# Rotated queries and keys of retention heads 1 to 3 from seven block products, and another order of the first loads

## The chip, the cores and the metric

The program runs on one core of one Trainium2 chip. Its time is the device time of one execution in microseconds (us). The core has a matrix engine (TensorE, PE in the profile; loading its stationary operand is PEld), VectorE (DVE), ScalarE (ACT), GpSimd (POOL) and SyncE (SP). SP, ACT and POOL issue the transfers between main memory and the on-chip memory; these run on 16 DMA engines. Matmul results go to PSUM, which is used here as eight tiles of 128 x 512 floats.

## The reference, cut to what matters

Two layers run over 512 tokens of width 1024. Each has a token-mixing part (dilated attention and a retention, both from one input projection of 11648 columns) and a feed-forward part. The change touches the queries and keys of the retention, four heads with 256 query and 256 key columns each:

```python
z = jnp.einsum('bsd,dc->bsc', x, w_in) + b_in          # the projection, 1024 deep
...
def rot(t):                                            # t: [B, S, H, 256]
    t1, t2 = t[..., :half], t[..., half:]
    return jnp.concatenate([t1 * cos - t2 * sin, t1 * sin + t2 * cos], axis=-1)
q = rot(q)
k = rot(k) * (dk ** -0.5)
...
sc = jnp.einsum('bhnd,bhmd->bhnm', qc, kc) * decay_mask
```

cos and sin depend on the token and on the index in the half (128 values). All of it is in float32.

## The kernel before, in words

**Numbers in two parts.** A float32 operand is held as a rounded high part and a low part that is the rest. `hilo` makes them: ACT casts the high part (L93), DVE subtracts it from the source for the low part (L94). A product of two such operands is three matmuls (`mm3`, all of them on L82): high by high, high by low, low by high. The input x stands transposed in `xh` and `xl`, eight blocks of 128 channels by 512 tokens; weights go from `raw` buffers (eight of 128 x 1024) into pairs `whi` and `wlo` (four of each).

**Direct products.** `wstat` makes 128 columns for all 512 tokens: eight channel blocks, three matmuls with 512 moving columns each. Its weights are cast by `unit` (L93, L94).

**Block products.** `Right`, `tall` and `wide` compute two column blocks from two weight blocks with seven products of half the depth and half the tokens in place of eight (Strassen's scheme in Winograd's form). x is cut in two halves of channels and two of tokens; sums of its blocks (S1 to S4) are made once per layer into `xs`. Of the weights, four blocks B11, B12, B21, B22 are combined: P1 and P3 are a load (SP) and then a transfer that adds a second block to it, issued by POOL (L321, `accum_op`), P2 and P4 are additions on DVE (L347). Each of the seven right operands is cast on ACT (L330) and subtracted on DVE (L336). `tall` has x stationary and 512 weight columns moving; `wide` has the weights stationary and 256 tokens moving, 24 matmuls to a product. After each product `ev(i, ps)` is called, which takes the partial results together. Three products accumulate in turn in one PSUM tile ("A" chain), so a later product there waits until the `ev` before it has read it:

```python
CHAIN = {1: "A", 6: "A", 7: "A", 4: "A", 2: "X", 5: "C", 3: "C"}
FIRST = (1, 2, 5)
WIDE = tuple(ORDER[i] for i in (0, 2, 4, 1, 5, 3, 6))   # products 1, 5, 6, 2, 7, 3, 4
```

`wide` is used before the change for the two branch gates and for most of the feed-forward part, `tall` for the values and gates of the retention.

**Retention.** For each head h: `rotary(h)` makes queries and keys (four `wstat`, L664) and rotates them on DVE (L668, L672, L673); `ret_values_gates(h)` is a `tall` of 512 value and 512 gate columns. Between the matmuls `tick` takes jobs from a list `side`: during `rotary(h)` the outputs of head h-1 (`one`: matmuls, a norm, then `turn`: transposes, a copy and a store), during values and gates the scores of head h. `one` needs a reciprocal root, for which POOL computes a power (L125) between two DVE instructions (L124, L126). `pace(20)` spreads the list over 20 us of estimated matmul time; `drain` runs what is left.

**The order of the work.** The program's text gives priorities; the order of each engine's instructions and of each queue is fixed when the kernel is built, by a planner that looks for what is ready by its own estimates of durations. On the chip each queue then runs in that fixed order.

**The start (layer 0).** Three warming matmuls; SP loads x in four tiles of 128 tokens and the first weights; x is transposed on PE (L170). The first matmuls (`wstat_halves`, tokens 0 to 255 first) need x tiles 0 and 1 and the first weights. POOL loads small tables, then cos and sin (L758, L759), then bias rows (L448, L451).

Of the kernel before, what the change touches and what calls it, by code (L numbers as in the profile page):

```python
# [14 lines left out]
ALU = mybir.AluOpType  # L15
# [38 lines left out]
def hybrid_kernel(ctx, tc, x, rel_bias, w_in, b_in, w_attn_proj, w_ret_proj, w_out,  # L54
# [582 lines left out]
    def layer(ly, cp):  # L637
# [16 lines left out]
        def slot(name="op", dt=F32R):  # L654
            return opp.tile([P, 2, S], dt, tag="op", name=name)

        def rotary(h):

            rot = []
            for c0 in (C_QR + h * RQ, C_KR + h * RQ):  # L660
                us = pair_units(w_l, c0)
                prod = []
                for t in range(2):
                    ps = wstat(us, t)  # L664
                    pr = []
                    for tb in (cos, sin):
                        m = work("rp")
                        dve.scalar_tensor_tensor(out=m, in0=ps, scalar=bcol(c0 + t * P), in1=tb, op0=ALU.add, op1=ALU.mult)  # L668
                        pr.append(m)
                    prod.append(pr)  # L670
                (t1c, t1s), (t2c, t2s) = prod
                dve.tensor_tensor(out=t1c, in0=t1c, in1=t2s, op=ALU.subtract)  # L672
                dve.tensor_tensor(out=t1s, in0=t1s, in1=t2c, op=ALU.add)  # L673
                pair = []
                for src in (t1c, t1s):
                    o_ = slot("rot")
                    hilo(src, o_[:, 0], o_[:, 1])
                    pair.append(o_)
                rot.append(pair)
            heads[h]["q"], heads[h]["k"] = rot  # L680

        def ret_values_gates(h):
            cv, cg = C_VR + h * RV, C_GR + h * RV
# [18 lines left out]
        with stage("attn") as ap_, stage("attw", 4) as aw:  # L702
            qk = {}

            def qk_slot(hp, g):
                qk[hp, g] = opp.tile([P, 2, S], F32, tag="op", name="qk")

            def qk_units(hp, g, how=pair_units):
                c = g * GW + hp * P
                return how(w_l, C_QA + c, C_KA + c)  # L710

            def qk_put(hp, g, j, ps):
                cc = (C_QA, C_KA)[j] + g * GW + hp * P
                o_, i_ = qk[hp, g][:, j], ps
                if g:
                    o_ = o_.rearrange("p (r l) -> p r l", r=4)
                    i_ = i_.rearrange("p (l r) -> p r l", r=4)
                dve.tensor_scalar(o_, i_, bcol(cc), (HD ** -0.5, 1.0)[j], op0=ALU.add, op1=ALU.mult)

            if ly == 0:  # L720
                x0 = [slot("x0", F32) for _ in range(NI)]
                warm = work("warm")
                dve.memset(warm, 0.0)
                px = psum()

                for _ in range(WARM):
                    mm(px, warm[:, :P], warm, True, True)
                act.dma_start(ident, c_id)

                def load_x(i):  # L730
                    for hf in range(2):
                        nc.sync.dma_start(x0[i][:, hf], x[i * P:(i + 1) * P, hf * S:(hf + 1) * S])

                load_x(0)
                load_x(1)
                for l_ in range(DEPTH):
                    pool.dma_start(braws[l_], b_in[l_].rearrange("(a b) -> a b", b=P))
                vecs = bias_vectors([aw.tile([P, S], F32, tag="bias", name="hot") for _ in range(NG)])
                first, make = qk_units(0, 0, pair_apart)
                load_x(2)  # L740
                cp = x_copies()
                late = []
                ops = [to_xT(x0[i].rearrange("p a b -> p (a b)"), i, cp, late if i < 2 else None) for i in range(NI)]
                for f in ops[0] + ops[1]:
                    f()
                make()
                for f in late:
                    f()
                us0 = [first, qk_units(0, 1)]
                load_x(3)  # L750
                side.extend([lambda l_=l_: bias_cols(l_) for l_ in range(DEPTH)] + vecs[:3] + ops[2] + vecs[3:] + ops[3])
                dve.tensor_tensor(out=pick, in0=ident[:, :NR], in1=ident[:, BK:BK + NR], op=ALU.add)
                rate[0], credit[0] = 0.4, 0.0
            else:
                us0 = [qk_units(0, g) for g in range(2)]
            for g in range(NG):
                qk_slot(0, g)
            pool.dma_start(cos, c_cos)  # L758
            pool.dma_start(sin, c_sin)  # L759
            if ly == 0:  # L760
                bias_rows()
            pss = wstat_halves([(us, j) for us in us0 for j in range(2)])
            drain()
            side.extend(x_sums(cp))
            pace(8)
            for n_, ps in enumerate(pss):
                qk_put(0, n_ // 2, n_ % 2, ps)
            us = qk_units(0, 2)
            for j in range(2):
                qk_put(0, 2, j, wstat(us, j))  # L770
            for t in range(2):
                c1, c2 = C_VA + t * VB, C_VA + (2 + t) * VB

                def put(i, s, c):
                    nc.sync.dma_start(v_d[i * P:(i + 1) * P, c - C_VA:c - C_VA + VB], s)

                def left(i, ps, s, c1=c1):
                    if s is None:
                        s = work("sn")[:, :VB]
                        act.copy(out=s, in_=ps)  # L780
                    else:
                        dve.tensor_tensor(out=s, in0=ps, in1=s, op=ALU.add)
# [24 lines left out]

            bias, tail = {}, []
            load_bias(0)
            for hp in range(HPG // 2):  # L810
                if hp:
                    for g in range(NG):
                        us = qk_units(hp, g)
                        qk_slot(hp, g)
                        for j in range(2):
                            qk_put(hp, g, j, wstat(us, j))
                    drain()
                ops, t_ = attention_pair(hp, [qk[hp, g] for g in range(NG)], load_v(hp), ap_, bias, yaT)
# [12 lines left out]
            for _ in range(4):  # L831
                next(vg)
            drain()

        with stage("ret") as rp:
            def ret_scores(h):
# [5 lines left out]
                def one(j):  # L842
                    n = S - j * P
                    ps = psum()[:, :n]
                    for d in range(2):
                        k_, q_ = heads[h]["k"][d], heads[h]["q"][d]
                        mm3(ps, k_[:, 0, j * P:(j + 1) * P], k_[:, 1, j * P:(j + 1) * P],
                            q_[:, 0, j * P:], q_[:, 1, j * P:], d == 0, d == 1)
                    t = work("pt")
                    dve.tensor_tensor(out=t[:, :n], in0=ps, in1=dec[:, :n], op=ALU.mult)  # L850
                    sl = heads[h]["p"][j]
# [354 lines left out]
```

## Time and profile before

| | |
|---|---|
| median of three runs | 2185.17 us (2185.1 to 2186.9) |
| the profiled execution | 2185.52 us, of it a span of 2183.7 us from first to last instruction |
| granted TensorE clock, mean | 0.997 |
| PE busy | 2161.5 us, 99% of the span |
| DVE busy | 1396.0 us, 64% |
| ACT busy | 980.6 us, 45% |
| POOL busy | 228.3 us, 10% |
| main memory read, written | 310.67 MB, 28.53 MB |

Busy times are sums of the durations of an engine's instructions where they overlap counted once. A matmul's record is longer than the distance to the next one, since they are pipelined: what a matmul costs in a run of them is read from the distance of their starts. Rows of the timeline give start, duration, engine, line, operation, output and inputs, and in brackets the idle time before it with what ended it. A row of the windows gives busy time and count for PE, PEld, DVE, ACT and POOL, then clock, DMA share and GB/s.

### The profile page before, as it was taken

The numbers are of one execution on the slowest core, as the hardware profiler recorded it, in microseconds if no ns is written. First come the engines' busy times: TensorE is split into PE (matmuls) and PEld (weight loads), VectorE is DVE, ScalarE is ACT, GpSimd is POOL, SyncE is SP. The second block draws the span as 40 slices with busy tenths as digits, with TensorE's granted clock in tenths as the row PEclk, the third lists the DMA queues.
The fourth block names the chain that finished last, engine by engine and source line by source line (L and its number), as shares of the span: only waits on it lengthen the run. The fifth ranks groups of instructions, "written<-read, shape, count | busy, mean of one in ns | idle before, by whom it ended". The sixth has DMA issues, their size and how long they took to land.

```text
span 2183.7 us, 32442 instructions
## 1 busy us (share of the span) xinstructions
PE 2161.5 (99%) x12906; PEld 1902.4 (87%) x12906; DVE 1396.0 (64%) x2011; ACT 980.6 (45%) x1585; POOL 228.3 (10%) x253
## 2 busy tenths in 40 slices
PE   8999999999999999999999999999999999999998
PEld 7977788889988899989898778888899889999996
DVE  5643677777755685747675346767877447766575
ACT  4444544546633263525245445444556233544350
POOL 4100011011000100010020000111010001000001
PEclk9999999999999999999999999999999999999999
DMA  8944266458685356656269343565577762666551
GB/s 230 235 134 104 59 164 164 135 131 194 190 305 192 88 154 132 171 133 158 93 163 255 89 92 92 140 178 148 137 188 227 260 193 58 175 151 161 125 161 39
DMA packets 304954, 338.60 MB, mean 155 GB/s; under 512 B 21790, under 2 KB 243138, under 8 KB 304673
## 3 DMA queue, kind: packets, MB, share of 16 engines
q1 hardware_dynamic: 227712, 248.81, 37.8%
q0 software_dynamic: 49808, 74.90, 18.1%
q10 hardware_dynamic: 27280, 12.80, 2.1%
q8 instruction: 101, 1.65, 0.3%
q14 instruction: 53, 0.43, 0.1%
HBM read 310.67 MB, written 28.53 MB: 155 GB/s over the span
## 4 chain that ended last, share of the span: by engine, by line
PE 90%; issue 4%; DMA 3%; DVE 2%; POOL 1%; ACT 0%; SPq 0%; POOLq 0%; DVEq 0%; ACTq 0%
PE ps L82 81%; PE px L82 7%; DMA raw<-in_w_in 2%; PE px L546 1%; DMA exd<-wb 1%; PE px L878 1%; POOL ry L125 0%; DMA mb<-exd 0%; DMA exd<-pk 0%; PE px L170 0%; DVE xtok L1001 0%; DVE wlo L336 0%; ACT whi L330 0%; PE px L602 0%; DVE xtok L1010 0%
## 5 line engine op out<-in xcount | busy, mean ns | idle before, releaser
L336 DVE TENSOR_TENSOR wlo<-raw,whi 128x1024 fp32r<-128x1024 f32 (+1 forms) x364 | 417.9, 1150 | 214.1 <-ACT whi L330 212.9
L82 PE MATMUL ps<-xh,whi 128*128 128x256 f32 (+1 forms) x1536 | 516.6, 338 | 4.5 <-ACT whi L93 3.5
L330 ACT CAST whi<-raw 128x1024 fp32r<-128x1024 f32 (+1 forms) x364 | 359.0, 990 | 345.4 <-PE ps L82 205.3
L82 PE MATMUL ps<-xh,wlo 128*128 128x256 f32 (+1 forms) x1536 | 500.9, 327 | 1.0 <-DVE wlo L94 1.0
L82 PE MATMUL ps<-xl,whi 128*128 128x256 f32 (+1 forms) x1536 | 501.2, 327 | 0.2 <-DVE xl L94 0.2
L82 PE MATMUL ps<-xs,whi 128*128 128x256 f32 (+1 forms) x2048 | 404.6, 296 | 0.0
L82 PEld LDWEIGHTS ps<-xs,whi 128*128 128x128 f32 x2048 | 327.7, 191 | 10.3
L94 DVE TENSOR_TENSOR wlo<-raw,whi 128x1024 fp32r<-128x1024 f32 (+2 forms) x162 | 193.3, 1196 | 202.0 <-ACT whi L93 201.0
L82 PEld LDWEIGHTS ps<-xh,whi 128*128 128x128 f32 x1536 | 292.4, 191 | 34.3 <-issue 5.7
L82 PEld LDWEIGHTS ps<-xh,wlo 128*128 128x128 f32 x1536 | 292.9, 191 | 26.5 <-DVE wlo L94 1.2
L82 PEld LDWEIGHTS ps<-xl,whi 128*128 128x128 f32 x1536 | 293.7, 191 | 19.5 <-DVE xl L94 1.0
L82 PE MATMUL ps<-xs,wlo 128*128 128x256 f32 (+1 forms) x1024 | 303.4, 296 | 0.0
L93 ACT CAST whi<-raw 128x1024 fp32r<-128x1024 f32 (+2 forms) x162 | 166.0, 1027 | 240.8 <-PE ps L82 150.7
L82 PE MATMUL ps<-whi,xs 128*128 128x512 f32 (+1 forms) x768 | 219.6, 360 | 0.6 <-ACT whi L330 0.4
L82 PEld LDWEIGHTS ps<-xs,wlo 128*128 128x128 f32 x1024 | 196.0, 191 | 5.0
L82 PE MATMUL ps<-whi,ht 128*128 128x512 f32 x576 | 178.4, 389 | 0.0
L82 PEld LDWEIGHTS ps<-whi,xs 128*128 128x128 f32 x768 | 137.7, 188 | 21.1 <-ACT sn L466 1.0
L82 PE MATMUL ps<-wlo,xs 128*128 128x512 f32 (+1 forms) x384 | 138.1, 360 | 0.8 <-DVE wlo L336 0.8
L321 POOL DMA_DIRECT2D raw<-in_w_in x64 | 79.2, 1263 | 472.9 <-DMA raw<-in_w_in 159.8
L82 PEld LDWEIGHTS ps<-whi,ht 128*128 128x128 f32 x576 | 108.2, 188 | 22.3
L321 POOL DMA_DIRECT2D raw<-in_w_ffn_gate x40 | 51.8, 1295 | 679.4 <-DMA raw<-in_w_ffn_up 251.4
L347 DVE TENSOR_TENSOR raw<-raw 128x1024 f32<-128x1024 f32 (+1 forms) x104 | 119.5, 1149 | 2.7 <-DMA raw<-in_w_in 0.5
(183 smaller groups left out, 2897.0 us busy)
## 6 DMA issues: line engine op xcount, KB each, us to landing
raw<-in_w_in SPq DMA_DIRECT2D x152, 512.0 KB, 4.3
raw<-in_w_ffn_up SPq DMA_DIRECT2D x64, 512.0 KB, 4.1
raw<-in_w_in POOLq DMA_DIRECT2D x48, 512.0 KB, 6.9
raw<-in_w_ffn_gate SPq DMA_DIRECT2D x44, 512.0 KB, 4.6
raw<-in_w_ffn_down SPq DMA_DIRECT2D x44, 512.0 KB, 4.2
raw<-in_w_ffn_gate POOLq DMA_DIRECT2D x40, 512.0 KB, 6.7
raw<-in_w_in SPq DMA_DIRECT2D x72, 256.0 KB, 4.9
raw<-in_w_ret_proj SPq DMA_DIRECT2D x32, 512.0 KB, 6.1
```

The source lines that it names most:

```text
L82: pe.matmul(ps, lhsT=a, rhs=b, start=start, stop=stop, skip_group_check=True)
L93: act.copy(out=hi, in_=src)
L94: dve.tensor_tensor(out=lo, in0=src, in1=hi.bitcast(F32), op=ALU.subtract)
L321: pool.dma_start(r, self.src({"P1": "B12", "P3": "B22"}[n], u), accum_op=ALU.add)
L330: act.copy(out=h, in_=src)
L336: dve.tensor_tensor(out=l, in0=src, in1=h.bitcast(F32), op=ALU.subtract)
L347: dve.tensor_tensor(out=r, in0=r, in1=self.t["B22" if n == "P2" else "B21", u], op=ALU.add)
L546: pe.transpose(px[:, (2 + j) * P:(3 + j) * P], s[:, hh, j * P:(j + 1) * P], ident)
L878: pe.transpose(px[:, t * P:(t + 1) * P], ys[i][:, t * P:(t + 1) * P], ident)
```

## The change

Queries and keys of heads 1, 2 and 3 of each layer are computed by one `wide` of seven products (weights of the queries are the one column block, those of the keys the other) in place of four `wstat`. Head 0 keeps its four `wstat`. The partial results are copied out of PSUM with the bias added on ACT, joined on DVE, and rotated in four quarters (queries or keys, tokens 0 to 255 or 256 to 511) by a new function `turned`. The rotated tiles are now kept as a high and a low tile of both halves, in place of a tile for each half; the scores read them accordingly.

At the start x tiles 2 and 3 are loaded after the first two groups of weights (before: tile 2 between them), and cos and sin go to SP's queue behind x in layer 0; in layer 1 they stay on POOL, ahead of three tile allocations.

```diff
+        def turned(t, ts_, hi, lo):
+            n = t.shape[2]
+            s = view(work("rs"), 2, n)
+            cs, sn_ = (a[:, ts_].unsqueeze(1).to_broadcast([P, 2, n]) for a in (cos, sin))
+            dve.tensor_tensor(out=s, in0=t, in1=sn_, op=ALU.mult)
+            dve.tensor_tensor(out=t, in0=t, in1=cs, op=ALU.mult)
+            dve.tensor_tensor(out=t[:, 0], in0=t[:, 0], in1=s[:, 1], op=ALU.subtract)
+            dve.tensor_tensor(out=t[:, 1], in0=t[:, 1], in1=s[:, 0], op=ALU.add)
+            hilo(t, hi[:, :, ts_], lo[:, :, ts_])
...
         def rotary(h):
...
+            cq, ck = C_QR + h * RQ, C_KR + h * RQ
+            for n_ in "qk":
+                heads[h][n_] = [slot("rot") for _ in range(2)]
+            if h == 0:
...
+            def biased_copy(ps, c, sign=1.0):
+                o_ = view(work("sn"), 2, 256)
+                for q in range(2):
+                    act.activation(out=o_[:, q], in_=ps[:, q * 256:(q + 1) * 256], func=AF.Identity, bias=bcol(c + q * P), scale=sign)
+                return o_
+
+            def ev(i, ps):
+                p2 = ps.rearrange("p (q t) -> p q t", q=2)
+                if i in (1, 5):
+                    sn[i] = biased_copy(ps, cq if i == 1 else ck)
+                elif i == 6:
+                    sn[i] = biased_copy(ps, ck, -1.0)
+                elif i == 2:
+                    dve.tensor_tensor(out=sn[1], in0=p2, in1=sn[1], op=ALU.add)
+                    turned(sn[1], slice(0, 256), *heads[h]["q"])
+                elif i == 7:
+                    dve.tensor_tensor(out=sn[5], in0=sn[5], in1=p2, op=ALU.subtract)
+                    turned(sn[5], slice(256, 512), *heads[h]["k"])
+                elif i == 3:
+                    dve.tensor_tensor(out=sn[6], in0=p2, in1=sn[6], op=ALU.add)
+                    turned(sn[6], slice(0, 256), *heads[h]["k"])
+                elif i == 4:
+                    turned(biased_copy(ps, cq), slice(256, 512), *heads[h]["q"])
+
+            wide(pair_right(w_l[:, :, cq:], w_l[:, :, ck:], 0), x_left, ev)
...
-                load_x(2)
                 cp = x_copies()
...
                 us0 = [first, qk_units(0, 1)]
+                load_x(2)
                 load_x(3)
+                nc.sync.dma_start(cos, c_cos)
+                nc.sync.dma_start(sin, c_sin)
...
             else:
                 us0 = [qk_units(0, g) for g in range(2)]
+                pool.dma_start(cos, c_cos)
+                pool.dma_start(sin, c_sin)
             for g in range(NG):
                 qk_slot(0, g)
-            pool.dma_start(cos, c_cos)
-            pool.dma_start(sin, c_sin)
```

More of the change, by code (lines that the diff above doesn't have):

```diff
@@ L655, in slot @@
             return opp.tile([P, 2, S], dt, tag="op", name=name)
-        def rotary(h):
[L659 to L680, printed above, removed]
+        def turned(t, ts_, hi, lo):
[7 more added lines that the diff above has]
+            hilo(t, hi[:, :, ts_], lo[:, :, ts_])
@@ new lines, in rotary @@
+        def rotary(h):
+            cq, ck = C_QR + h * RQ, C_KR + h * RQ
+            for n_ in "qk":
+                heads[h][n_] = [slot("rot") for _ in range(2)]
+            if h == 0:
+                for c0, n_ in ((cq, "q"), (ck, "k")):
+                    us = pair_units(w_l, c0)
+                    prod = []
+                    for t in range(2):
+                        ps = wstat(us, t)
+                        pr = []
+                        for tb in (cos, sin):
+                            m = work("rp")
+                            dve.scalar_tensor_tensor(out=m, in0=ps, scalar=bcol(c0 + t * P), in1=tb, op0=ALU.add, op1=ALU.mult)
+                            pr.append(m)
+                        prod.append(pr)
+                    (t1c, t1s), (t2c, t2s) = prod
+                    dve.tensor_tensor(out=t1c, in0=t1c, in1=t2s, op=ALU.subtract)
+                    dve.tensor_tensor(out=t1s, in0=t1s, in1=t2c, op=ALU.add)
+                    for t, src in enumerate((t1c, t1s)):
+                        hilo(src, heads[h][n_][0][:, t], heads[h][n_][1][:, t])
+                return
+            sn = {}
+            def biased_copy(ps, c, sign=1.0):
[21 more added lines that the diff above has]
+            wide(pair_right(w_l[:, :, cq:], w_l[:, :, ck:], 0), x_left, ev)
@@ L845, in one @@
                     for d in range(2):
-                        k_, q_ = heads[h]["k"][d], heads[h]["q"][d]
-                        mm3(ps, k_[:, 0, j * P:(j + 1) * P], k_[:, 1, j * P:(j + 1) * P],
-                            q_[:, 0, j * P:], q_[:, 1, j * P:], d == 0, d == 1)
+                        (kh, kl), (qh, ql) = ([t_[:, d] for t_ in heads[h][n_]] for n_ in "kq")
+                        ks = slice(j * P, (j + 1) * P)
+                        mm3(ps, kh[:, ks], kl[:, ks], qh[:, j * P:], ql[:, j * P:], d == 0, d == 1)
                     t = work("pt")
```

## Prediction

> **What bounds the kernel.** I read the page first, then who PE waited for, then the windows of one retention head. The first fence shows the busy times and, of the chain that ended last, the shares by engine; the second PE's waits; the third three windows: the rotary of head 2, its values and gates, and one product group of the feed-forward part that already runs as `wide`.
>
> ```profile
> PE 2161.5 (99%) x12906; PEld 1902.4 (87%) x12906; DVE 1396.0 (64%) x2011; ACT 980.6 (45%) x1585; POOL 228.3 (10%) x253
> ...
> PE 90%; issue 4%; DMA 3%; DVE 2%; POOL 1%; ACT 0%; SPq 0%; POOLq 0%; DVEq 0%; ACTq 0%
> ```
>
> ```profile
> PE ps L82 <- ACT whi L93: 3.5, 2, 2.1
> ```
>
> ```profile
> 361.86:392.10 30.24, 30.24 (x142) 25.02 (x141) 21.11 (x44) 10.53 (x15) 7.07 (x8) 1.00 0.78 178
> 392.10:435.37 43.27, 43.27 (x199) 36.06 (x197) 33.19 (x41) 24.68 (x33) 0.62 (x1) 1.00 0.43 125
> 872.30:892.40 20.10, 20.10 (x169) 20.10 (x169) 15.14 (x16) 10.84 (x15) 2.56 (x2) 1.00 0.80 184
> ```
>
> PE is the bound nearly everywhere: it is idle for 2183.7 - 2161.5 = 22 us of the span, its longest group of waits is 3.5 us, and inside the retention head it never stops. So a matmul less is time less, as long as the others keep up. DVE is the nearest follower: 21.11 of 30.24 us in the rotary, 33.19 of 43.27 in values and gates, together 54.3 of 73.5 us (74%).
>
> **PE's share of the change.** What a matmul costs here is the distance of starts. The rows are one `wstat` stretch (512 columns, twelve matmuls between them) and one `wide` product (256 columns, 24 matmuls).
>
> ```profile
> 387.80 0.39 PE L82 MATMUL ps<-xh,whi 128*128 128x512 f32 x1
> ...
> 390.53 0.60 PE L878 MATMUL px<-ident,yb 128*128 128x128 f32 x4
> ...
> 566.41 0.28 PE L82 MATMUL ps<-xh,whi 128*128 128x256 f32 x1
> ...
> 569.29 0.40 PE L82 MATMUL ps<-xs,whi 128*128 128x256 f32 x2
> ```
>
> (390.53 - 387.80)/12 = 0.2275 us, and (569.29 - 566.41)/24 = 0.120 us, so two halves cost 5% more than a whole. Removed for a head: 4 `wstat` x 8 x 3 = 96 matmuls, 21.84 us. Added: 7 x 24 = 168, 20.16 us. Saved 1.68 us for a head, **10.1 us** for the six (heads 1 to 3, two layers). The jobs of the list between them are unchanged; the stage goes from 30.2 to 28.5 us.
>
> The Trainium skill ("TensorE: Matmul & The Clock Gate", section "Back-to-back issue gap") gives a warm gap of N/2.4 + 2.5 ns: 215.8 ns for 512 columns and 109.2 for 256. By it a head would save 96 x 0.2158 - 168 x 0.1092 = 2.37 us, six 14.2, and the time would be 4 us lower than mine (an estimate from that page). The rows above measure 227.5 and 120 in this kernel, with a weight load before each matmul, so I keep 10.1.
>
> **DVE's share.** The steps between starts on DVE, from the rows below: 512 columns 0.60 to 0.66 us, 256 columns 0.33, 1024 columns 1.14 to 1.15, and the norm of one `one` job 2.3 us (449.55 to 451.86).
>
> ```profile
> 393.22 0.74 DVE L668 SCALAR_TENSOR_TENSOR rp<-ps,bT,sin 128x512 f32<-128x512 f32 x1
> 393.88 0.68 DVE L673 TENSOR_TENSOR rp<-rp 128x512 f32<-128x512 f32 x1
> 394.48 0.68 DVE L672 TENSOR_TENSOR rp<-rp 128x512 f32<-128x512 f32 x1
> 395.08 1.22 DVE L336 TENSOR_TENSOR wlo<-raw,whi 128x1024 fp32r<-128x1024 f32 x1
> 396.22 1.28 DVE L94 TENSOR_TENSOR rot<-rp,rot 128x512 fp32r<-128x512 f32 x2
> 398.23 1.22 DVE L336 TENSOR_TENSOR wlo<-raw,whi 128x1024 fp32r<-128x1024 f32 x1 [0.72 <-ACT whi L330]
> 399.49 1.23 DVE L347 TENSOR_TENSOR raw<-raw 128x1024 f32<-128x1024 f32 x1
> 400.63 1.22 DVE L336 TENSOR_TENSOR wlo<-raw,whi 128x1024 fp32r<-128x1024 f32 x1
> ...
> 351.47 0.41 DVE L850 TENSOR_TENSOR pt<-px,dec 128x256 f32<-128x256 f32 x1
> 351.80 1.22 DVE L336 TENSOR_TENSOR wlo<-raw,whi 128x1024 fp32r<-128x1024 f32 x1
> ...
> 449.55 0.69 DVE L868 BATCH_NORM_STATS2 st<-px 128x6 f32<-128x512 f32 x1
> ...
> 451.86 1.22 DVE L336 TENSOR_TENSOR wlo<-raw,whi 128x1024 fp32r<-128x1024 f32 x1
> ```
>
> Weights: 4 low parts become 7, and P2 and P4 are two additions: 5 x 1.145 = +5.7 us. Rotation, before: 8 x 0.66 + 8 x 0.60 = 10.1 us. After: three joins of 0.60 and four `turned` of 2 x 0.60 + 2 x 0.33 + 0.60 = 2.46 us, 11.6 us. In all +7.2 us a head, 61.5 of 71.8 us (86%). That fits on average; the question is the end of the stage. Its products end, with the `one` and `turn` jobs that the list puts between them (0.68, 1.37, 2.05 and 2.73 us of matmuls, from 3, 6, 9 and 12 of 0.2275), at about 3.6, 7.8, 13, 18.7, 21.9, 25.1 and 28 us. The first three need only a copy on ACT; the joins and rotations hang on the last four. So from 18.7 to 28.4 us DVE has the last norm (2.3), three rotations with joins (9.2) and three low parts (3.4), 14.9 us of work in 9.7: 5.2 us are left over, and the fourth rotation comes to it (2.5), 7.7 us past the end of the stage. Before, what was left after the end (392.1) were the rows from 392.5 to 397.5 without the low part at 395.08: 3.8 us. So the low parts of values and gates come up to **3.9 us later** than before. How much that may be, the next rows say: the first uses of the two low parts that end at 399.45 and 401.85.
>
> ```profile
> 404.21 0.40 PE L82 MATMUL ps<-wlo,xs 128*128 128x512 f32 x1
> ...
> 405.58 0.39 PE L82 MATMUL ps<-wlo,xs 128*128 128x512 f32 x1
> ```
>
> Their slack is 4.8 and 3.7 us, so nearly all of the delay is covered and 0 to 0.2 us is not. One more place is tight: product 4 (the last) goes to the PSUM tile that the join after product 7 reads. Product 7 ends at 21.9, DVE comes to that join after the last norm and the rotation of product 2 (18.7 + 2.3 + 3.1 = 24.1, 25.2 with a low part between), is done at 25.8, and PE wants the tile at 25.1. I take **0.5 us** of stall for a head from both places, 3.0 for six; the bounds are 0 (the planner fits the low parts into the pauses, as it does at 395.08, where one stands before the subtractions of the rotation) and, if nothing of the 3.9 us is covered, 23 us for six.
>
> **Hidden costs.** The rows for ACT are its casts, its activation nearest to the new copies, and a table load; those for transfers the two queues of the page.
>
> ```profile
> L330 ACT CAST whi<-raw 128x1024 fp32r<-128x1024 f32 (+1 forms) x364 | 359.0, 990 | 345.4 <-PE ps L82 205.3
> ...
> L927 ACT ACTIVATE sg<-ps,bT 128x256 f32<-128x256 f32 x16 | 6.7, 469 | 2.7 <-PE ps L82 2.7
> L698 ACT ACT_TABLE_LOAD x2 | 2.6, 1283 | 0.0
> ...
> q1 hardware_dynamic: 227712, 248.81, 37.8%
> q0 software_dynamic: 49808, 74.90, 18.1%
> ```
>
> ACT gets three more casts of 990 ns and eight copies of 256 columns; by the gates' activation of 469 ns that is 6.7 us more beside 10.5 busy of 30, behind PE. That the copy (Identity) would need a table load cannot be excluded; a load takes 1283 ns by its row, on ACT alone, with 20 us free. Transfers: 2 MB of weights for a head become 2.5 MB by SP and 1 MB that POOL's queue adds. By the queue rows (37.8% of 2183.7 us for 248.81 MB is 3.3 us a MB, 18.1% for 74.90 is 5.3) that is 7 us more DMA time in a head that uses 0.78 x 30.2 + 0.43 x 43.3 = 42 of 73.5 us now. They are issued in the second half of values and gates, where the share is 0.43; if that cover failed, the first products of the rotary would wait for them.
>
> **The start.** The rows: SP's issues, POOL's, the chain's step to the first weights, the window of that step (its last number is GB/s), and PE's transposes of x tiles 2 and 3.
>
> ```profile
> 2.61 2.98 SPq L220 DMA_DIRECT2D raw<-in_w_in  x4
> 5.64 3.38 SPq L732 DMA_DIRECT2D x<-in_x  x4
> 9.06 12.51 SPq L211 DMA_DIRECT2D raw<-in_w_in  x8
> ...
> 4.62 0.58 POOL L758 DMA_DIRECT2D cos<-const_cos  x1
> ...
> 3.64 8.80 DMA raw<-in_w_in
> ...
> 13.14 0.50 PE ps L82 x2
> ...
> 3.64:12.44 8.80, 6.02 (x23) 3.41 (x22) 3.85 (x7) 3.08 (x6) 6.60 (x12) 1.00 1.03 302
> ...
> 28.34 1.97 PE L170 MATMUL px<-ident,x 128*128 128x128 f32 x16
> ```
>
> PE's first long run begins at 13.14, because the third part of the first weights, issued at 3.64, needs 8.80 us to land. cos and sin (512 KB) are in the air beside it, from 4.62. Moved behind all x tiles on SP, they leave it alone: at the rate of that window, which is close to 0.3 MB in a us, it is worth at most 1.7 us; nothing, if other transfers fill the place at once. I take **1.0 us** less. The x tiles 2 and 3, now behind the second weights, are issued some 3.3 us later; they are not transposed before 28.34, so that is covered; uncovered it would cost 3 us. The second weights, at 9.06 today, come earlier. POOL's bias rows move up by a us, and nobody waits for them. In layer 1 nothing of weight moves.
>
> **Sum.** Against the profiled execution's own time of 2185.52 us: -10.1 (PE) +3.0 (stalls) -1.0 (start) = 2177.4; that execution is 0.35 above the median of the runs, so 2177.
>
> **Rivals.**
> 1. *The stall takes the gain.* If the tail of each rotary stalls PE by 1.5 us more than I allow (2 us a head instead of 0.5), 10.1 turns into -2: about 2184 to 2186, no change. For it speaks 86% load and a tail of 14.9 us of work in 9.7; against it the measured slack of 3.7 to 4.8 us.
> 2. *POOL holds DVE (slower).* The planner's order is fixed, and POOL's queue now has the two adding transfers of each rotary and, later than before, the four of values and gates, among the powers for the norms. Behind such a transfer a power already came late:
>
> ```profile
> 374.15 1.20 POOL L321 DMA_DIRECT2D raw<-in_w_in  x1 [4.69 <-issue]
> 374.90 1.04 POOL L125 TENSOR_TENSOR ry<-ve,mhalf 128x1 f32<-128x1 f32 x1
> ...
> 375.98 0.22 DVE L126 SCALAR_TENSOR_TENSOR rt<-ry,ve 128x1 f32<-128x1 f32 x1 [6.04 <-POOL ry L125]
> ```
>
> DVE stood 6.0 us there, with everything behind L126. In the middle of the stage, as now, it costs PE nothing. If the hold falls after 18.7 us into the stage, where my sum spends all slack, PE loses it whole: with 4.5 us a head 27 us, 2177 + 27 = 2204; at half of the heads 2190. It decides from 1.4 us a head on ((10.1 + 1.0 - 3.0)/6). The last norm's matmuls stand just ahead of that point, and the values' loads are later because five of the eight `raw` buffers are taken by the rotary instead of four; against it, the planner sees the same queue.
> 3. *All of it covered.* No stall and the whole 1.7 us at the start: 2185.2 - 11.8 = 2173.
> 4. *The change does not save on PE*, because single 256-column matmuls between jobs run slower than in the pure `wide` stretches: at 0.130 us they would cost the same 21.84. The window at 872 us is a `wide` at 169 matmuls in 20.1 us, with few jobs between. About 2185 to 2188 with the stalls.
>
> **How the numbers follow.** Forecast 0.50, rival 1 0.18, rival 2 0.19, rival 3 0.08, rival 4 0.05. 0.2% (4.4 us) is about what a measurement of this kernel can tell from no change. Faster: forecast and rival 3, 0.58; same: rival 1 and most of 4, 0.22; slower 0.20. The likeliest case alone would lie in 2173 to 2181 (stall 0 to 1.2 us a head); to hold 8 in 10 the range is 2172 to 2192, which takes in rivals 1, 3 and 4 and the half case of rival 2.
>
> **What would show it.** Right: the rotary of head 2 as 168 matmuls of 256 columns at 0.120 us, the stage near 28.5 us, DVE above 80% there with rows of rotation running past its end, PE waits on DVE of some 0.5 us a head on the "A" tile or on the first low parts of values and gates; the first long PE run before 12.5 us. Wrong: PE waits of over 1.4 us a head, with L125 or L126 as the row just ahead (rival 2) or with low parts late and POOL free (rival 1); a `wide` step of 0.13 us (rival 4); first products waiting for an adding transfer, which I put at nothing; PE's start unmoved.

## The result, and the profile after

The changed kernel takes **2198.97 us** (median of five runs, 2195.73 to 2202.05); before, beside it, 2185.33 (2185.10 to 2188.08). The ratio is 1.006 with an interval of 1.0047 to 1.0074: slower by about 13.6 us, where 8 faster were forecast. The profiled execution is the median one, with a span of 2197.2 us, 13.5 longer than before.

First the page of the kernel after: its busy times, and of the chain that ended last the shares by engine.

```profile
PE 2158.1 (98%) x13338; PEld 1918.4 (87%) x13338; DVE 1436.3 (65%) x2083; ACT 1018.9 (46%) x1651; POOL 242.7 (11%) x263
...
PE 83%; DVE 6%; issue 4%; DMA 4%; POOL 1%; ACT 1%; SPq 0%; POOLq 0%; DVEq 0%; ACTq 0%
```

PE does have less to do (2158.1 us in place of 2161.5), but it now stands idle for 2197.2 - 2158.1 = 39 us in place of 22, and in the chain PE has lost seven points, most of them to DVE. What PE waits for is in the view of waits (us in total, times, longest), kernel after:

```profile
PE ps L82 <- DVE wlo L336: 13.5, 11, 3.2
PE ps L82 <- ACT whi L93: 3.9, 3, 1.5
PE px L917 <- ACT yb L912: 3.2, 3, 1.5
```

The first has grown from 0.8 us and the third is new; before, the longest group was 3.5 us, on the high parts. L336 makes the low parts of the block products' weights; L917 is the transposition of a head's normed output, which runs when the list of jobs is drained after the rotary. These two are 16.7 us together; PE's idle time has grown by 16.9.

Where the time is lost, head by head: the table takes the first score matmul of each retention head (before and after, from PE's timeline) and shows how much later it comes than before. The last row is what was lost or won from one head to the next.

| | layer 0: head 0 | head 1 | head 2 | head 3 | layer 1: head 0 | head 1 | head 2 | head 3 |
|---|---|---|---|---|---|---|---|---|
| before, us | 274.23 | 342.98 | 416.48 | 489.99 | 1354.47 | 1423.17 | 1496.64 | 1570.11 |
| after, us | 276.13 | 347.21 | 421.35 | 498.23 | 1362.95 | 1434.53 | 1508.67 | 1584.09 |
| later by | 1.90 | 4.23 | 4.87 | 8.24 | 8.48 | 11.36 | 12.03 | 13.98 |
| from the head before | | +2.33 | +0.64 | +3.37 | | +2.88 | +0.67 | +1.95 |

The six heads lose 11.84 us together, where each should have won 1.68. The stretch ahead of head 0 loses 1.90; all the rest of two layers, with the feed-forward parts, moves by less than half a us.

The wait itself, in head 2. First PE's timeline of the kernel after, with the first products of values and gates; then three rows of POOL's timeline from the end of the rotary ahead of them, and SP's issue of the load that the second adding transfer adds to; then DVE's.

```profile
396.47 0.39 PE L82 MATMUL ps<-whi,xh 128*128 128x512 f32 x1
...
397.97 0.50 PE L82 MATMUL ps<-wlo,xh 128*128 128x512 f32 x1 [1.12 <-DVE wlo L336]
...
404.59 0.50 PE L82 MATMUL ps<-wlo,xh 128*128 128x512 f32 x1 [0.65 <-DVE wlo L336]
```

```profile
383.35 1.22 POOL L321 DMA_DIRECT2D raw<-in_w_in  x1 [3.41 <-DMA raw<-in_w_in]
389.65 1.19 POOL L321 DMA_DIRECT2D raw<-in_w_in  x1 [5.08 <-DVE sn L709]
390.40 1.04 POOL L125 TENSOR_TENSOR ry<-ve,mhalf 128x1 f32<-128x1 f32 x1
```

```profile
383.92 0.37 SPq L110 DMA_DIRECT2D raw<-in_w_in  x1
```

```profile
388.53 0.68 DVE L709 TENSOR_TENSOR sn<-sn,ps 128x512 f32<-128x512 f32 x1
...
391.48 0.22 DVE L126 SCALAR_TENSOR_TENSOR rt<-ry,ve 128x1 f32<-128x1 f32 x1 [2.27 <-POOL ry L125]
...
396.69 1.22 DVE L336 TENSOR_TENSOR wlo<-raw,whi 128x1024 fp32r<-128x1024 f32 x1
```

Read from the bottom: the low part that PE wants at 396.85 is made on DVE from 396.69 to 397.91. DVE is late because it stood 2.27 us in front of L126, which needs the power of the last norm. POOL does that power at 390.40, because an adding transfer stands ahead of it in POOL's order, and POOL can issue that transfer only at 389.65, after 5 us of waiting. (The row's bracket names L709 on DVE. What the transfer needs is its load: issued at 383.92, it took 5.1 us and landed at 389.05.) That is rival 2 of the prediction, with all three of its parts: transfer, power, DVE. The holds of all six heads are in DVE's timeline of the kernel after, at L126 of the last norm of each head:

```profile
317.38 0.22 DVE L126 SCALAR_TENSOR_TENSOR rt<-ry,ve 128x1 f32<-128x1 f32 x1 [4.02 <-POOL ry L125]
...
391.48 0.22 DVE L126 SCALAR_TENSOR_TENSOR rt<-ry,ve 128x1 f32<-128x1 f32 x1 [2.27 <-POOL ry L125]
...
464.38 0.22 DVE L126 SCALAR_TENSOR_TENSOR rt<-ry,ve 128x1 f32<-128x1 f32 x1 [1.02 <-POOL ry L125]
...
472.30 0.69 DVE L662 TENSOR_TENSOR rs<-sn,sin 128x512 f32<-128x512 f32 x1 [3.22 <-DMA y_d<-yt]
...
1404.69 0.22 DVE L126 SCALAR_TENSOR_TENSOR rt<-ry,ve 128x1 f32<-128x1 f32 x1 [4.51 <-POOL ry L125]
...
1478.80 0.22 DVE L126 SCALAR_TENSOR_TENSOR rt<-ry,ve 128x1 f32<-128x1 f32 x1 [2.28 <-POOL ry L125]
...
1554.26 0.22 DVE L126 SCALAR_TENSOR_TENSOR rt<-ry,ve 128x1 f32<-128x1 f32 x1 [3.59 <-POOL ry L125]
```

Six heads, six holds, each near the end of its rotary and each behind an adding transfer in POOL's timeline; in head 3 of layer 0 there is a second one of 3.22 us, in front of the multiplication by the sine, whose work buffer still feeds the store of an output (`y_d<-yt`). Together 20.9 us.

What the matmuls cost is in PE's timeline of the kernel after, inside the new `wide`:

```profile
379.65 0.28 PE L82 MATMUL ps<-xh,whi 128*128 128x256 f32 x1
...
381.69 0.28 PE L82 MATMUL ps<-xh,wlo 128*128 128x256 f32 x1
```

Seventeen steps in 2.04 us are 0.120 us a step, as in the feed-forward part. Last the two stages of head 2 as windows of the kernel after (rotary, from its first matmul; values and gates, up to the next rotary):

```profile
366.09:394.77 28.68, 28.68 (x215) 27.42 (x214) 21.46 (x45) 13.76 (x22) 7.10 (x8) 1.00 0.77 176
394.77:440.24 45.47, 43.71 (x199) 35.82 (x198) 39.59 (x53) 27.56 (x39) 3.19 (x3) 1.00 0.61 161
```

PE is busy throughout the rotary, which takes 28.7 us (28.5 were forecast), and has lost 1.76 us in the stage behind it. The damage is done in one stage and paid in the next.

### The profile page after: what moved, and what is told of

It is laid out like the page before. It is cut to its first block, busy times and chain, and to the rows that moved or that the text cites. A ratio compares the mean times of both kernels' runs of the same rounds, so it can differ in the third digit from the quotient of the medians.

```text
span 2197.2 us, 33517 instructions
## 1 busy us (share of the span) xinstructions
PE 2158.1 (98%) x13338; PEld 1918.4 (87%) x13338; DVE 1436.3 (65%) x2083; ACT 1018.9 (46%) x1651; POOL 242.7 (11%) x263
## 4 chain that ended last, share of the span: by engine, by line
PE 83%; DVE 6%; issue 4%; DMA 4%; POOL 1%; ACT 1%; SPq 0%; POOLq 0%; DVEq 0%; ACTq 0%
PE ps L82 75%; PE px L82 6%; DMA raw<-in_w_in 2%; DVE wlo L336 1%; PE px L546 1%; DMA exd<-wb 1%; POOL ry L125 1%; DVE sn L663 1%; DVE rs L662 0%; DMA y_d<-yt 0%; DVE rot L94 0%; PE px L170 0%; DMA mb<-exd 0%; DVE xtok L1040 0%; DMA exd<-pk 0%
## 5 line engine op out<-in xcount | busy, mean ns | idle before, releaser
L336 DVE TENSOR_TENSOR wlo<-raw,whi 128x1024 fp32r<-128x1024 f32 (+1 forms) x406 | 469.3, 1158 | 213.2 <-ACT whi L330 210.5
L330 ACT CAST whi<-raw 128x1024 fp32r<-128x1024 f32 (+1 forms) x406 | 403.4, 996 | 380.0 <-PE ps L82 211.0
L82 PE MATMUL ps<-xh,whi 128*128 128x256 f32 (+1 forms) x1488 | 481.4, 325 | 4.9 <-ACT whi L93 3.9
L82 PE MATMUL ps<-xs,whi 128*128 128x256 f32 (+1 forms) x2432 | 476.9, 295 | 0.0
L82 PE MATMUL ps<-xh,wlo 128*128 128x256 f32 (+1 forms) x1488 | 467.2, 315 | 1.0 <-DVE wlo L94 1.0
L82 PE MATMUL ps<-xl,whi 128*128 128x256 f32 (+1 forms) x1488 | 467.6, 315 | 0.2 <-DVE xl L94 0.2
L82 PEld LDWEIGHTS ps<-xs,whi 128*128 128x128 f32 x2432 | 388.3, 192 | 11.5
L82 PE MATMUL ps<-xs,wlo 128*128 128x256 f32 (+1 forms) x1216 | 358.2, 295 | 0.0
L94 DVE TENSOR_TENSOR wlo<-raw,whi 128x1024 fp32r<-128x1024 f32 (+2 forms) x138 | 164.2, 1192 | 194.1 <-ACT whi L93 193.8
L82 PEld LDWEIGHTS ps<-xs,wlo 128*128 128x128 f32 x1216 | 232.9, 192 | 4.9
```

Of the source, the lines that this page charges most:

```text
L82: pe.matmul(ps, lhsT=a, rhs=b, start=start, stop=stop, skip_group_check=True)
L94: dve.tensor_tensor(out=lo, in0=src, in1=hi.bitcast(F32), op=ALU.subtract)
L330: act.copy(out=h, in_=src)
L336: dve.tensor_tensor(out=l, in0=src, in1=h.bitcast(F32), op=ALU.subtract)
```

## Experiments

Two theories stood at the outset. **H (hold):** the time goes to the powers that stand on POOL behind a waiting adding transfer; DVE, which waits in a fixed order, is late with the next low parts. **W (work):** DVE has too much to do (7.2 us more a head, and a tail that spills into the next stage), and would be late without any hold. Beside them stands the start, which could have cost something too.

### The start alone, and the block products alone

The kernel before with the new order of the first loads only:

```diff
                 first, make = qk_units(0, 0, pair_apart)
-                load_x(2)
...
                 us0 = [first, qk_units(0, 1)]
+                load_x(2)
                 load_x(3)
+                nc.sync.dma_start(cos, c_cos)
+                nc.sync.dma_start(sin, c_sin)
...
                 us0 = [qk_units(0, g) for g in range(2)]
+                pool.dma_start(cos, c_cos)
+                pool.dma_start(sin, c_sin)
...
-            pool.dma_start(cos, c_cos)
-            pool.dma_start(sin, c_sin)
```

> The kernel before with the new order of the first loads alone; queries and keys as before. In the changed kernel PE reaches the same instructions 1.3 us later by 54 us into the span, with a new wait of 1.2 us at 20.0 and a second half-clock stretch of 3.4 us. If the order of the loads causes that: 1 to 2.5 us above the kernel before (2186 to 2188). If the prediction's step was right and the block products cost it: 1 us below (2184).

Measured: 2187.86 us beside 2186.29 for the kernel before, ratio 1.0005 (0.9995 to 1.0015): no difference that can be told.

The changed kernel with those lines taken back to the old order:

> The changed kernel with the old order of the first loads. If the slowdown is that of the block products: 11 to 13 us above the kernel before (2196 to 2199). If the start had a share beyond its own 1.3 us, by what it shifts later: under 2194.

Measured: 2201.50 us, ratio 1.0068 (1.0053 to 1.0083), 2.5 us above the range that was expected. PE's waits in that kernel:

```profile
PE ps L82 <- DVE wlo L336: 14.4, 11, 3.5
```

So the loss is all in the block products; the start neither makes it nor mends it.

### No power on POOL

In the outputs of the retention the power is replaced by a copy on DVE. It leaves a computation out: the outputs of the heads are scaled by a factor made from the variance itself, in place of its reciprocal root. All loads and adding transfers stay; but in these norms DVE no longer waits for POOL.

```diff
-        pool.tensor_tensor(out=y, in0=ve, in1=mhalf, op=ALU.pow)
+        if on_pool:
+            pool.tensor_tensor(out=y, in0=ve, in1=mhalf, op=ALU.pow)
+        else:
+            dve.tensor_copy(y, ve)
...
-                    rs = rstd_of(mv[:, 1:2])
+                    rs = rstd_of(mv[:, 1:2], False)
```

> The changed kernel, with POOL's power in the norms of the retention's outputs replaced by a copy on DVE, in all eight heads; the output scale is left wrong by that, the number of DVE instructions is one more for each norm. No DVE instruction then waits for POOL, while the adding transfers stay. Theory hold (POOL's last power stands behind the last adding transfer and holds DVE 1.0 to 4.5 us near the end of each rotary): PE's waits on low parts and on the last transposes, 18 us with the half clock, go nearly away: 2180 to 2187. Rival load (DVE has simply more work at the end of the rotary than it can do): the waits stay at over 1.2 us a head: 2190 to 2197.

Measured: 2177.20 us, ratio 0.9960 (0.9945 to 0.9975), where the changed kernel has 1.006: some 22 us less, and 3 us below what the expectation had for the hold. PE's waits on these low parts are all but gone:

```profile
PE ps L82 <- DVE wlo L339: 0.4, 1, 0.4
```

Head by head, from the same first score matmuls as above: -1.77, -1.74, -1.75, and in layer 1 three times -1.71. That is the saving on PE with nothing taken from it, -10.39 us for six. Against the kernel after, the heads gain 4.10, 2.38, 5.12, 4.59, 2.38 and 3.66 us; the holds were 4.02, 2.27, 4.24 (1.02 + 3.22), 4.51, 2.28 and 3.59. **Each us that DVE was held cost PE a us**, to about 0.1 us in five heads; in head 3 of layer 0 the loss is 0.9 us more (the last section shows PE at half clock there). Where in the stage the hold falls decides: another hold in the kernel after, of 1.35 us and 13 us before the one at 1404.69, cost nothing. Theory W falls: DVE still has all its added work here. Since the edit also leaves the planner free to order other things anew, the next one tests the same by another way, with the computation whole.

### The last block loaded ahead of the sum

In the values and gates the loads of the second operands are issued as B11, B21, P1, P3, B22. P1 and P3 each need an adding transfer behind a plain load. Here B22 goes ahead of P3:

```diff
-        return Right(src, [(k, n) for k in nk])
+        return Right(src, [(k, n) for k in nk], loads=("B11", "B21", "P1", "B22", "P3"))
```

> The changed kernel with the weights of values and gates loaded in the order B11, B21, P1, B22, P3, so that the adding transfers of P3 stand behind the last power on POOL's queue; all values as in the changed kernel. Theory hold: DVE's wait for POOL at the end of the rotary falls under 1 us and the time to 2181 to 2189, unless P3 then comes late for its own product. Rival load: 2193 to 2199.

Measured: 2176.89 us, ratio 0.9957 (0.9942 to 0.9971), below the range that was expected for the hold. The mechanism, in POOL's timeline of this kernel at head 2 (its lines are one higher than before, so the power is L126 and the adding transfer L322), from the last norm on, and behind it two rows of DVE's, the input of the last power (`ve`) and the instruction that uses it:

```profile
381.34 0.55 POOL L126 TENSOR_TENSOR ry<-ve,mhalf 128x1 f32<-128x1 f32 x1 [7.48 <-DMA raw<-in_w_in]
385.69 1.22 POOL L322 DMA_DIRECT2D raw<-in_w_in  x1 [3.80 <-DMA raw<-in_w_in]
394.29 1.20 POOL L322 DMA_DIRECT2D raw<-in_w_in  x1 [7.38 <-ACT rot L94]
```

```profile
381.11 0.15 DVE L125 TENSOR_SCALAR ve<-mv 128x1 f32<-128x1 f32 x1
...
381.93 0.22 DVE L127 SCALAR_TENSOR_TENSOR rt<-ry,ve 128x1 f32<-128x1 f32 x1
```

Both adding transfers of P3 now come behind the last power, which starts as soon as its input is there (381.11 + 0.15; the row's bracket names a load, which POOL was not behind). POOL still waits 3.8 and 7.4 us for them, but nothing on DVE is behind those waits, and L127 follows without one. PE's waits on the block products' low parts are down to one, and the two stages of head 2 as windows of this kernel:

```profile
PE ps L83 <- DVE wlo L337: 1.2, 1, 1.2
```

```profile
360.00:388.67 28.67, 28.67 (x215) 27.42 (x214) 23.71 (x50) 15.61 (x24) 5.87 (x7) 1.00 0.64 156
388.67:432.02 43.35, 43.35 (x199) 35.89 (x198) 37.43 (x48) 25.80 (x36) 4.37 (x4) 1.00 0.73 183
```

DVE is busy for 23.71 + 37.43 = 61.1 of 72.0 us, 85%, and PE does not stop. The amount of work was not the limit.

### The load order in the kernel before

Is the load order worth something by itself? The kernel before with the same one line:

> The kernel before with only the load order of values and gates changed to B11, B21, P1, B22, P3. In the kernel before PE does not stop in the rotary, although DVE waits for POOL in its middle. Theory hold (the load order helps only by taking a hold away that meets the end of the rotary): no change, 2184 to 2188. If that load order is worth 20 us by itself in another way: under 2180.

Measured: 2184.07 us, ratio 0.9993 (0.9983 to 1.0002): no difference that can be told. In the kernel before every one of the six heads has a hold of DVE by POOL, of 1.4 to 7.5 us, 29.8 together (the 6 us that the prediction shows are one of them). With the line none over 0.8 us is left in these heads, and the time is the same. Those holds end 13 to 16 us into a rotary of 30 and cost PE nothing, so nothing is won by taking them away. The line is worth something only with the change.

### Block products, new load order, old start

The block products and the new load order of values and gates, with the first loads in the order of the kernel before:

> Block products with the load order B11, B21, P1, B22, P3 for values and gates, and the old order of the first loads. By the two looks so far (start order: no difference that can be told; load order: 22 us off the changed kernel): 2175 to 2178, as the same kernel with the new order of the first loads.

Measured: 2174.33 us, ratio 0.9939 (0.9925 to 0.9954), just below what was expected.

### More work for DVE

If DVE's amount of work has room, more of it should cost little. The kernel with B22 first, and the first multiplication of each `turned` issued twice, four of 0.60 us or 2.4 us a head:

```diff
             dve.tensor_tensor(out=s, in0=t, in1=sn_, op=ALU.mult)
+            dve.tensor_tensor(out=s, in0=t, in1=sn_, op=ALU.mult)
```

> The kernel with the new load order of values and gates, with the first multiplication of each rotated quarter issued twice on DVE: 4 x 0.60 = 2.4 us more of DVE work a head, three of the four at the end of the rotary, same values. If the prediction's reckoning of the slack is right (3.9 us of delay against 3.7 to 4.8 us of slack, all spent): up to 2.4 us of PE waits a head, 2185 to 2192. If DVE's amount of work is not what binds: 2176 to 2180.

Measured: 2176.35 us, ratio 0.9954 (0.9940 to 0.9969), as without it. The six heads win 8.09 us against the kernel before (7.99 without the added work), and PE waits for low parts as little as ever:

```profile
PE ps L82 <- DVE wlo L336: 0.5, 2, 0.2
```

So 2.4 us of further work a head costs nothing that can be seen, while a hold of 2.27 us cost 2.38. That the planner, which knows the work, puts low parts ahead of it, and doesn't foresee the hold, would explain it; no run shows what it estimated.

### The jobs placed earlier

The changed kernel with the jobs beside the rotary spread over 14 us in place of 20, which moves the last norm away from the end of the stage:

```diff
                 if h:
-                    pace(20)
+                    pace(14)
                     rotary(h)
```

> The changed kernel with the list of the rotary paced over 14 us in place of 20: the last norm is done earlier in the stage, the last adding transfer of values and gates then stands behind the last power on POOL's queue, the third ahead of it. Load order and DVE work as in the changed kernel. Theory hold: DVE waits at the end of the rotary under 1 us, 2176 to 2186. Rival load: the same total of work, shifted from the end of the rotary to its middle by 2.3 us: 2188 to 2197.

Measured: 2201.26 us, ratio 1.0055 (1.0035 to 1.0075). That is above both ranges of the expectation. The order on POOL came out as it was expected, the third adding transfer ahead of the last power and the fourth behind it; but the third too was late, and DVE was held by it for 2 us and more in place of under 1. POOL's timeline of this kernel at head 1, then DVE's:

```profile
312.30 1.20 POOL L321 DMA_DIRECT2D raw<-in_w_in  x1 [9.05 <-issue]
313.05 1.05 POOL L125 TENSOR_TENSOR ry<-ve,mhalf 128x1 f32<-128x1 f32 x1
```

```profile
314.14 0.22 DVE L126 SCALAR_TENSOR_TENSOR rt<-ry,ve 128x1 f32<-128x1 f32 x1 [5.95 <-POOL ry L125]
```

The holds of the six heads were 5.95, 2.21, 2.00, 2.08, 5.54 and 2.00 us, 19.8 together, and the time is that of the changed kernel. The six heads lie 30.4 us above the kernel without the power, more than the holds: PE went to half clock six times in them, which the last section prices at 1.7 us each. The run does not separate the two theories, since the holds stayed, and it does not tell how long before the end of the stage a hold would be harmless; it shows again that where there is a hold of this length near the end, the time is lost.

### The start again, with the hold gone

The two kernels with B22 first, with the old and with the new start, five rounds each on one chip:

> Block products, new load order of values and gates, old order of the first loads; the kernel of c2 again, beside the next on one chip. 2173 to 2177. If the new order of the first loads costs something: below the next by 1 to 3 us; if not, the two intervals lie over each other.

> The same with the new order of the first loads, the kernel of e4 again: 2174 to 2179.

Measured: old start 2177.00 us, ratio 0.9955 (0.9942 to 0.9967); new start 2175.47 us, 0.9949 (0.9935 to 0.9962), beside 2185.28 for the kernel before. The intervals overlap: the start makes no difference that can be told. Either version **beats both kernels**, the one before by some 8 to 10 us here and by 9 to 12 in the earlier runs, about 0.5%.

One loss of the same kind is left. In the profiled execution with the old start, head 1 of layer 0 lost 2.09 us where the same kernel won 1.25 in the profile of the section on the old start above: ACT stood 3.87 us in front of a copy, until the store of an output (`y_d<-yt`) had read the copy's buffer, DVE then stood 2.06 us for ACT, and PE 1.93 us for the low part (at 326.78). That store landed 7.6 us after its issue, 5.8 in the other profile.

## Why the prediction was wrong, step by step

**PE's matmuls: right.** Forecast -10.1 us for six heads at 0.120 us a step; with the hold taken away they win 10.4. The profiles of the kernels with B22 first, which leave nothing out, keep 6.0 to 8.1 of it (6.0 where the store came late). Rival 4 (a slower `wide` step) is out. The gap formula of the Trainium skill's page "TensorE: Matmul & The Clock Gate", section "Back-to-back issue gap", would have had 14.2 us; the Trainium skill gives it there for a matmul by itself and says that a stream with weight loads differs, and the 10.4 measured here does not agree with it.

**DVE's amount of work: right; the slack was reckoned too tight.** 86% was forecast, 85% is the row of the kernel with B22 first, without a stop on PE there. The reckoning that low parts come late by up to 3.9 us and that almost all of it is covered gave DVE too little room: 2.4 us more a head cost nothing. It also took the slack from the third product of values and gates (`wlo,xs` in its rows); where PE did wait in the kernel after, it was in the first two (`wlo,xh`).

**The stall: this is the step that failed.** The sum had 0.5 us a head for it, 3.0 in all; it measured 3.7 a head. The kernel after lies 22.2 us above the one without the power in these heads. The stall was costed from the amount of work on DVE, with DVE never standing still, and the hold by POOL was put aside as a rival with a chance of 0.19. As a mechanism rival 2 was exact: the transfer ahead of a power, the hold late in the stage, the loss of its whole length, and the point from which it decides, 1.4 us a head (a head's holds were 2.3 to 4.5). Its price was between its two cases: 2190 with half of the heads, 2204 with 4.5 us in all, 2199 measured, with an average of 3.5. Only the 3.22 us behind the store's work buffer in one head are not in it; they went with the power too. The other tight place that the sum named, the "A" tile, shows no wait of PE in the kernel after. What was wrong was the sentence that spoke against it, "the planner sees the same queue". The planner had already let DVE stand 6.04 us in the kernel before, in a row that the prediction shows. That hold was evidence that the planner does not avoid such an order, not that it finds a harmless place for it.

What could have warned of it in the profile of before is arithmetic on POOL's queue. There the four adding transfers for values and gates of head 2 stood at 362.46, 364.36, 368.25 and 374.15, the last 12.3 us into the rotary, which starts at 361.86, and the second of the four powers was behind it. In the kernel after they stand at 375.10, 377.48, 383.35 and 389.65, the last 23.6 us into a stage that starts at 366.09; behind it is the last power. The rotary's own two adding transfers are not among them: they are issued in the stage before, at 345.25 and 349.75, as forecast. It is the loads that moved: by the view of waits SP stood 5.2 us for a low part on DVE (L336), which frees a `raw` buffer, before it issued the one at 383.92. Rival 2 had this ("later than before, the four of values and gates"), and the sum did not move the hold by it.

**The start: half right, worth nothing.** SP's timeline of the kernel after, then PE's first long run and the next wait:

```profile
2.59 2.13 SPq L220 DMA_DIRECT2D raw<-in_w_in  x4
...
4.77 4.15 SPq L769 DMA_DIRECT2D x<-in_x  x4
...
8.96 0.44 SPq L788 DMA_DIRECT2D cos<-const_cos  x1
...
9.74 0.33 SPq L789 DMA_DIRECT2D sin<-const_sin  x1
...
10.91 11.27 SPq L211 DMA_DIRECT2D raw<-in_w_in  x8
```

```profile
11.59 0.58 PE L82 MATMUL ps<-xh,whi 128*128 128x256 f32 x1 [1.49 <-ACT whi L93]
...
20.01 0.39 PE L82 MATMUL ps<-xh,whi 128*128 128x256 f32 x1 [1.21 <-ACT whi L93]
```

PE's first run begins at 11.59 in place of 13.14, 1.55 us earlier where 1.0 was forecast (12.36 in the kernel with the start alone, 12.31 in the one with B22 first). But "the second weights, at 9.06 today, come earlier" is wrong: the text asks for them ahead of x tiles 2 and 3, the planner's order has all of x, cos and sin ahead, and they are issued from 10.91. The prediction read the program's text as the order of SP's queue, though the rows of before already gave the planner's order and not the text's. PE waits 1.21 us for the second weights at 20.01, and that is not all. The windows from PE's first run to its wait for the third tile of x, kernel before and then after:

```profile
13.14:30.65 17.51, 17.17 (x117) 15.02 (x117) 6.40 (x11) 6.27 (x11) 5.87 (x12) 0.90 0.65 175
```

```profile
11.59:20.01 8.42, 7.22 (x47) 7.01 (x47) 1.70 (x5) 3.61 (x6) 3.97 (x8) 0.82 1.10 317
20.01:31.93 11.92, 11.58 (x70) 9.43 (x70) 4.79 (x7) 2.66 (x5) 1.50 (x3) 0.86 0.30 80
```

They are the same 117 matmuls, in 17.51 us before and in 20.34 after. The lower clock (the last number but two) makes up most of the rest: 0.10 of 17.51 is 1.75 us lost before, 0.18 of 8.42 and 0.14 of 11.92 are 3.18 after. So the 1.55 us are gone, and PE is 1.28 us later than before at 31.93. In the kernel with the start alone it is 0.56 us earlier at that wait (30.09), and in the one with B22 first 0.19 later (30.84). None of this is visible in the times. "Nobody waits for them", of POOL's bias rows, held in the kernel after but not in every kernel: PE waited 3.5 us for them (at 13.60) in the block products with the old start, and 1.6 us (at 18.76) in the second profile of the new start with B22 first.

Where the rest of the 1.90 us ahead of head 0 comes from stays open. There the start alone has 2.25, the block products alone 1.50, and the first two profiles with B22 first have none (-0.18 and -0.28); it moves with every reordering, and was not followed further.

**The cover of the transfers held.** No new wait of PE is on an adding transfer itself, as forecast. The loads were late for POOL, and it is the order behind them that mattered.

## What to carry to other kernels

Where an engine's queue carries transfers that wait for loads and also small operations on which another engine waits, treat every such operation as costing up to the longest wait ahead of it, and look where in the stage that falls: in slack it is free, at the end of a stage it is lost in full. A hold in the profile of before that costs nothing is a warning, because a change that moves the loads or the jobs moves the hold too. Here one line in the order of the loads turned a loss of 13.6 us into a gain of some 10.

## What the runs showed of the hardware

**Half clock after short waits.** In head 3 of layer 0 PE waited 3.18 us (at 474.18). The windows behind it, kernel after (after the busy times of the five engines come clock, DMA share and GB/s):

```profile
474.70:475.20 0.50, 0.50 (x3) 0.39 (x3) 0.50 (x2) 0.00 (x0) 0.00 (x0) 1.00 1.05 294
475.20:476.00 0.80, 0.80 (x4) 0.63 (x3) 0.80 (x3) 0.00 (x0) 0.00 (x0) 0.66 1.03 165
476.00:477.50 1.50, 1.50 (x5) 1.21 (x4) 1.50 (x4) 0.86 (x2) 0.00 (x0) 0.50 0.84 305
477.50:478.50 1.00, 1.00 (x4) 0.72 (x4) 1.00 (x2) 0.24 (x1) 0.00 (x0) 0.50 0.07 25
478.50:479.00 0.50, 0.50 (x3) 0.41 (x2) 0.50 (x2) 0.31 (x1) 0.00 (x0) 0.64 0.00 0
```

About 1.3 us after PE has started again the clock goes to half. A mean of 0.66 over 0.80 us is 0.54 us at half, then 1.50 and 1.00, then 0.64 over 0.50 is 0.36: 3.4 us in all, which cost 1.7. The Trainium skill's page "TensorE: Matmul & The Clock Gate", section "What's actually happening", has a table of the two states by which the clock goes to half after an idle window of about 3.4 us. The 3.4 us at half agree with that figure, but the wait ahead was shorter than it, and in the kernel with the jobs placed earlier 2 us were enough. PE's timeline there, with one wait that led to a drop and one that didn't, and the windows behind them:

```profile
408.14 0.50 PE L82 MATMUL ps<-wlo,xh 128*128 128x512 f32 x1 [2.02 <-DVE wlo L336]
...
1477.96 0.44 PE L917 MATMUL px<-ident,yb 128*128 128x128 f32 x2 [1.84 <-ACT yb L912]
```

```profile
409.00:411.50 2.50, 2.50 (x7) 1.97 (x6) 2.50 (x4) 1.00 (x2) 0.00 (x0) 0.50 0.00 0
...
1478.50:1481.00 2.50, 2.28 (x20) 2.07 (x18) 2.12 (x3) 1.87 (x3) 0.00 (x0) 1.00 1.09 192
```

In that kernel's retention six waits of 1.93 to 2.54 us were each followed by a drop; the one of 1.84 us was not. In the retention of the kernel after, waits of up to 1.64 us stayed without one. It is no sharp threshold, since a wait of 1.75 us (at 199.57 of the kernel with the jobs placed earlier) had a drop behind it, and so had the 1.21 us at 20.01 of the kernel after, whose clock is this two us later:

```profile
22.00:24.00 2.00, 2.00 (x11) 2.00 (x11) 1.23 (x1) 0.08 (x1) 0.50 (x1) 0.50 0.72 203
```

A stall of 2 us can so cost 3.7.
